# The down projections of a two-layer encoder: eleven chunk pairs by seven products instead of two whole chunks and ten pairs

## The chip, the cores and the metric

One core of a Trainium2 chip runs the whole program in one launch. The metric is the device time of one execution in microseconds (us). The engines are named as in the profile: PE is the matrix engine (PEld its weight loads), DVE the vector engine, ACT the scalar engine, POOL the GpSimd engine; SP issues most DMA transfers, POOL issues those that add into their target.

## The reference

Two layers over 512 tokens of width 1024. Each layer has two gated feed-forward half steps, a mixer between them (banded and dilated attention in the even layer, neighbourhood attention in the odd one), and a gated per-layer input at its end; a last norm follows.

```python
D_MODEL = 1024; SEQ = 512; DEPTH = 2; D_FF = 2816
def swiglu(x, w_gate, w_up, w_down):
    return (jax.nn.silu(x @ w_gate) * (x @ w_up)) @ w_down
...
for i in range(DEPTH):
    h = h + 0.5 * swiglu(rmsnorm(h, norm_ffn1[i]), ffn1_w_gate[i], ffn1_w_up[i], ffn1_w_down[i])
    hn = rmsnorm(h, norm_mix[i])
    h = h + (ab_mixer(hn, ...) if i % 2 == 0 else c_mixer(hn, ...))
    h = h + 0.5 * swiglu(rmsnorm(h, norm_ffn2[i]), ffn2_w_gate[i], ffn2_w_up[i], ffn2_w_down[i])
    gate = jax.nn.sigmoid(rmsnorm(h, norm_ple[i]) @ w_ple_gate[i])
    h = h + gate * (p[i] @ w_ple_proj[i])
return rmsnorm(h, norm_final)
```

All is float32. The change concerns the last matrix product of `swiglu`, 512 x 2816 by 2816 x 1024, which occurs four times. These four places are called the down stages here.

## The kernel before

**Number format.** A float32 operand is split into a high and a low part (`split`, lines 152 to 154): ACT copies it to the narrower matmul type (line 153) and DVE subtracts that copy from it (line 154). A product of two operands is then three matmuls: high by high, high by low, low by high. Each of them has a 128 x 128 stationary operand and here 512 moving columns. So every weight tile costs one ACT copy and one DVE subtraction before PE can use it. In the profile a split weight tile is `wh` and `wl`, a raw one is `wr` (1024 columns, 512 KB) or `tmp` (512 columns, 256 KB), an activation is `act`.

**A feed-forward half step.** `ffn` makes the 22 chunks of 128 hidden features: two in `front`, then four in each of five calls of `block`. `block` leaves its rows with tokens on the partitions; `turn_back` transposes them on PE (line 449) and ACT copies each transposed chunk out of its bank (line 450) into the list `a`. A block's chunks are turned during the next block (`between`), those of the last block inside the down stage (`turn`).

**The down stage** (`down`) multiplies the 22 chunks with the down weights. Of the 22, the first `WHOLE = 2` are multiplied plainly (`xs`, the weight halves `left` and `right`). The other 20 make `K2 = 10` pairs `A[k]`, `B[k]`. A pair is a 2 x 2 block product: tokens in two halves `l` and `r` of 256, the pair's two chunks, and the 1024 outputs in two halves of 512, so the weights of all pairs are four quarters `b11`, `b12`, `b21`, `b22`. Seven products stand in the place of eight, at the price of sums and differences of the operands and results: `inner_sums` (lines 496 to 498) and line 594 on the activations; on the weights the DMAs that add (`add`, line 533) and DVE adds in `summed` (line 567). One product of one pair is six matmuls: two banks of 128 tokens, three each.

Pairs go in units of two (`units`), five units before. The products are named `first` to `seventh`. Each unit's weights pass through a chain: `first` uses `b11`, then `b12` is added in place for `fifth`; later `summed` loads `b12` plus `b22` for `seventh`, `b11` is added for `sixth`, `b21` for `fourth`. `second` uses `b21` and `third` uses `b22`, loaded into `tmp` tiles (`halved`). The stage runs in this order:

- the whole chunks' right half for tokens `r` into the two transposition banks (`rx`); their weights and splits were prepared in the last block (`late`);
- a loop over the units `s`: `first(s)`, `second(s)`, and from `s = 2` on `fifth(s - 2)`. At `s = 1` the last four chunks are turned, through the two score banks, two around `second(1)` and two behind it;
- `summed(0)`, `seventh(0)`, the whole chunks' left half for tokens `l`, `summed(1)`, the last two `fifth`, the left half for tokens `r`;
- a loop `s = 1` to 6: `summed(s + 1)`, `seventh(s)`, `sixth(s - 1)`, `fourth(s - 2)`, at `s = 2` the whole chunks' right half for tokens `l`, at the end `third(0)`;
- `third(1)` to `third(4)`, between them the transposition of finished quarters, the addition to the residual (lines 683 and 693) and the split of the next norm's input (`norm_split`, lines 216 and 217); the last quarter follows `third(4)` (line 707 and line 693). The next stage's products read these splits.

**Order.** The instructions of an engine stand in the order of a scheduler that goes by the order of the program text, by which tile slots are free and by its own estimate of when operands are ready; so products can stand interleaved or be moved ahead. `issue_after(x)` keeps what it encloses behind `x` on `x`'s engine. `high_priority` moves instructions ahead. Each engine then runs its own list strictly in order. Slots: five `wr`, ten `tmp`, four `wh` and four `wl` tiles, 64 `act` tiles; PSUM has three `mm` banks, two `sc`, two `tr`, one `ob`.

Of the kernel before, what the change touches and what calls it, by code (L numbers as in the profile page):

```python
# [10 lines left out]
F32R = mybir.dt.float32r  # L11
# [4 lines left out]
P = 128  # L16
# [20 lines left out]
WHOLE = 2  # L37
READY = 8
K2 = (NF - WHOLE) // 2
# [16 lines left out]
class Trunk:  # L56
# [259 lines left out]
    def block(self, w, y, t, between, late, start):  # L316
# [90 lines left out]
        def fifth():  # L407
            for i in both:
                tt(base[i], base[i], chain[i], op=ALU.add)  # L409
            late()  # L410
# [43 lines left out]
    def ffn(self, i, which, k_next):  # L454
# [6 lines left out]
        a, xs, x1, sums, begin = [], [None] * WHOLE, [None] * K2, [None] * K2, []  # L461
# [3 lines left out]
        def between():  # L465
            a.extend(self.turn_back(rows, self.tbank))
            for k in range(READY):
                if WHOLE + 2 * k + 2 <= len(a) and sums[k] is None:
                    sums[k] = self.inner_sums(*a[WHOLE + 2 * k:WHOLE + 2 * k + 2])

        def late():
            if j == BLOCKS - 1:
                for n, x in enumerate(a[:WHOLE]):
                    xs[n] = self.split_chunk(x, nc.vector)
                for k in range(WHOLE):
                    begin.append(self.tmp())
                    nc.sync.dma_start(begin[k], dn[:, (WHOLE + k) * T:(WHOLE + k + 1) * T])

        for j in range(BLOCKS):
            n = 4 * UNIT + j * 8 * UNIT  # L480
            rows = self.block(gu[:, n:n + 8 * UNIT], y, t, between, late, first and j == 0)
        self.begin_norm(k_next)
        p = lambda: [self.per_layer(i, c) for c in range(2)]
        self.down(dn, a, xs, x1, sums, begin, kept, p if which == 2 else None, lambda n: a.extend(self.turn_back(rows, self.sbank, n)))
# [16 lines left out]
    def down(self, w, a, xs, x1, sums, begin, kept, inner, turn):  # L501
# [7 lines left out]
        A, B = _Step(a, WHOLE), _Step(a, WHOLE + 1)  # L509
        left, right = (w[:, n * WHOLE * T:(n + 1) * WHOLE * T] for n in range(2))  # L510
        b11, b12, b21, b22 = (w[:, 2 * WHOLE * T:][:, n * K2 * T:(n + 1) * K2 * T] for n in range(4))
        units = [range(u, min(u + 2, K2)) for u in range(0, K2, 2)]
        wide = [range(u, u + 2) for u in range(0, WHOLE, 2)]
# [39 lines left out]
        r1, r2 = [self.bank(), self.bank()], [self.bank(), self.obank()]  # L553
# [3 lines left out]

        rx = [self.tbank(), self.tbank()]
        for u in wide:
            product(rx, u, halved(right, u, begin[u.start:u.stop]), xs, r, True, u.stop == WHOLE)  # L560

        def summed(s):
            raws[s] = load(b12, units[s])
            for j, k in enumerate(units[s]):
                x, more = raws[s][:, j * T:(j + 1) * T], self.tmp()
                nc.sync.dma_start(more, b22[:, k * T:(k + 1) * T])
                tt(x, x, more, op=ALU.add)

# [11 lines left out]
        def second(s):  # L580
            u = units[s]
            for k in u:
# [1065 lines left out]
```

## Time and profile before

| | |
|---|---|
| three runs | 2004.49, 2005.36, 2005.66 us; median 2005.36 |
| the profiled execution | 2005.77 us; its span from first to last instruction 2003.9 us |
| mean granted PE clock | 0.997 |
| busy | PE 1976.0, PEld 1646.1, DVE 1537.0, ACT 1213.0, POOL 324.7 us |
| matmuls | 9726 |
| DMA | 346.12 MB, mean 173 GB/s |

Times inside the profile count from the first instruction of the span. A row of the timeline gives start, duration, engine, line, operation, tiles, shape and count; in brackets at its end stands how long the engine sat idle before it and what ended that. Consecutive matmuls overlap in their durations (0.39 us each for 512 columns), so what one costs PE is read from the distance of their starts. The same holds, less strongly, for DVE and ACT. The four down stages begin at 230.0, 859.1, 1251.7 and 1817.2 us.

### The profile page before, as it was taken

What the parts mean: (1) busy time and instruction counts of PE and PEld (TensorE: products, weight loads), DVE (VectorE), ACT (ScalarE), POOL (GpSimd) and SP (SyncE); (2) the same over time, 40 slices, a digit from 0 to 9 for tenths busy, and PEclk for the clock granted to TensorE, in tenths of its full rate; (3) what the DMA queues carried; (4) which work ended last, traced back from release to release, by engine and by line L of the source; (5) the groups of instructions that cost most, each with busy time, mean ns of one, the idle gap of its engine ahead of it and who ended that gap; (6) DMA issues with size and microseconds to landing.
All of it is one profiled execution on the core that took longest, in us unless ns stands there. A gap on an engine that the chain in (4) does not pass through costs nothing.

```text
span 2003.9 us, 28013 instructions
## 1 busy us (share of the span) xinstructions
PE 1976.0 (99%) x9726; PEld 1646.1 (82%) x9726; DVE 1537.0 (77%) x2648; ACT 1213.0 (61%) x2051; POOL 324.7 (16%) x378
## 2 busy tenths in 40 slices
PE   9999999999999999999999999999999999999997
PEld 7888788879888888878888888788888888887886
DVE  7787897798767677797786778877888668778775
ACT  7656765477645565675566556745766556666553
POOL 1111011341211221111122110011000122110111
PEclk9999999999999999999999999999999999999999
DMA  9877687543426787878568786785343577776961
GB/s 274 196 198 174 170 213 225 141 95 78 96 73 221 173 184 173 195 188 222 189 214 186 178 190 168 209 212 162 104 129 100 188 181 188 176 173 177 230 222 43
DMA packets 151069, 346.12 MB, mean 173 GB/s; under 512 B 26384, under 2 KB 34064, under 8 KB 150928
## 3 DMA queue, kind: packets, MB, share of 16 engines
q1 hardware_dynamic: 112704, 236.28, 36.0%
q0 software_dynamic: 38080, 108.02, 30.5%
q8 instruction: 76, 1.25, 0.2%
q14 instruction: 65, 0.53, 0.1%
q10 hardware_dynamic: 144, 0.04, 0.0%
HBM read 315.96 MB, written 17.27 MB: 166 GB/s over the span
## 4 chain that ended last, share of the span: by engine, by line
PE 87%; DVE 5%; DMA 3%; issue 3%; ACT 2%; POOL 0%; DVEq 0%; ACTq 0%; POOLq 0%
PE mm L368 7%; PE mm L369 7%; PE mm L367 7%; PE mm L178 5%; PE mm L180 5%; PE mm L179 5%; PE sc L367 3%; PE sc L369 3%; PE sc L368 3%; PE mm L544 3%; PE mm L542 3%; PE mm L543 3%; PE sc L543 2%; PE sc L544 2%; PE sc L542 2%
## 5 line engine op out<-in xcount | busy, mean ns | idle before, releaser
L153 ACT ACTIVATE wh<-wr 128x1024 fp32r<-128x1024 f32 (+1 forms) x408 | 427.2, 1050 | 424.2 <-DMA wr<-in_gu_dram 82.3
L154 DVE TENSOR_TENSOR wl<-wr,wh 128x1024 fp32r<-128x1024 f32 (+1 forms) x408 | 496.2, 1219 | 199.5 <-ACT wh L153 197.0
L367 PE MATMUL mm<-wh,act 128*128 128x512 f32 x640 | 250.9, 392 | 0.0
L369 PE MATMUL mm<-wh,act 128*128 128x512 f32 x640 | 250.7, 392 | 0.0
L368 PE MATMUL mm<-wl,act 128*128 128x512 f32 x640 | 249.5, 390 | 0.6 <-DVE wl L154 0.5
L153 ACT ACTIVATE wh<-tmp 128x512 fp32r<-128x512 f32 x264 | 155.6, 625 | 95.8 <-PE sc L369 32.6
L178 PE MATMUL mm<-act,wh 128*128 128x512 f32 (+1 forms) x472 | 184.8, 393 | 0.4 <-ACT act L153 0.4
L179 PE MATMUL mm<-act,wh 128*128 128x512 f32 (+1 forms) x472 | 184.5, 391 | 0.0
L180 PE MATMUL mm<-act,wl 128*128 128x512 f32 (+1 forms) x472 | 184.4, 391 | 0.0
L154 DVE TENSOR_TENSOR wl<-tmp,wh 128x512 fp32r<-128x512 f32 x264 | 171.5, 683 | 4.1 <-ACT wh L153 3.7
L337 POOL DMA_DIRECT2D wr<-in_gu_dram x80 | 80.4, 1020 | 379.8 <-DVE wl L154 360.6
L368 PEld LDWEIGHTS mm<-wl,act 128*128 128x128 f32 x640 | 120.2, 188 | 25.7 <-DVE wl L154 1.5
L369 PEld LDWEIGHTS mm<-wh,act 128*128 128x128 f32 x640 | 120.2, 188 | 24.4
L367 PEld LDWEIGHTS mm<-wh,act 128*128 128x128 f32 x640 | 120.3, 188 | 23.8
L154 DVE TENSOR_TENSOR act<-act,act 128x512 fp32r<-128x512 f32 (+1 forms) x216 | 133.8, 634 | 3.8 <-ACT act L153 3.7
L153 ACT ACTIVATE act<-act 128x512 fp32r<-128x512 f32 (+1 forms) x216 | 120.7, 582 | 24.0 <-DVE act L311 9.9
L367 PE MATMUL sc<-wh,act 128*128 128x512 f32 x320 | 124.6, 389 | 1.6 <-DVE act L291 1.6
L369 PE MATMUL sc<-wh,act 128*128 128x512 f32 x320 | 124.7, 390 | 0.0
L368 PE MATMUL sc<-wl,act 128*128 128x512 f32 x320 | 124.5, 389 | 0.0
L409 DVE TENSOR_TENSOR wr<-wr,wr 128x1024 f32<-128x1024 f32 x40 | 49.0, 1225 | 87.8 <-DMA wr<-in_gu_dram 87.6
L533 POOL DMA_DIRECT2D wr<-in_dn_dram x60 | 51.9, 864 | 365.9 <-DVE wl L154 325.3
L345 POOL DMA_DIRECT2D tmp<-in_gu_dram x80 | 74.8, 1200 | 221.8 <-DVE act L498 137.0
(272 smaller groups left out, 4631.3 us busy)
## 6 DMA issues: line engine op xcount, KB each, us to landing
wr<-in_gu_dram SPq DMA_DIRECT2D x92, 512.0 KB, 5.2
tmp<-in_gu_dram SPq DMA_DIRECT2D x160, 256.0 KB, 3.7
wr<-in_gu_dram POOLq DMA_DIRECT2D x80, 512.0 KB, 7.6
tmp<-in_dn_dram SPq DMA_DIRECT2D x144, 256.0 KB, 4.0
wr<-in_dn_dram POOLq DMA_DIRECT2D x60, 512.0 KB, 6.3
tmp<-in_gu_dram POOLq DMA_DIRECT2D x80, 256.0 KB, 5.9
wr<-in_dn_dram SPq DMA_DIRECT2D x40, 512.0 KB, 4.4
act<-kept SPq DMA_DIRECT2D x56, 256.0 KB, 4.5
```

What stands on the lines that cost most here:

```text
L153: self.put(self.nc.scalar.activation(hi, src, AF.Copy))
L154: self.put((lo_eng or self.nc.vector).tensor_tensor(lo, src, hi.bitcast(F32), op=ALU.subtract))
L178: mm(out, stat[0], mov[0], start=start, stop=False)
L179: mm(out, stat[0], mov[1], start=False, stop=False)
L180: return mm(out, stat[1], mov[0], start=False, stop=stop)
L337: nc.gpsimd.dma_start(raw, q[:, u * UNIT:(u + 1) * UNIT], accum_op=ALU.add)
L367: mm(p, xh, wh, start=start and k == 0, stop=False, skip_group_check=True)
L368: mm(p, xh, wl, start=False, stop=False, skip_group_check=True)
L369: self.last_mm = mm(p, xl, wh, start=False, stop=stop and k == half - 1, skip_group_check=True)
L542: mm(p, xh, wh, start=start and k == 0, stop=False, skip_group_check=True)
L543: mm(p, xh, wl, start=False, stop=False, skip_group_check=True)
L544: ins = mm(p, xl, wh, start=False, stop=stop and k == u.stop - 1, skip_group_check=True)
```

## The change

All 22 chunks become pairs: `WHOLE` is gone, `K2` is 11, and there are six units, the last with a single pair. With the whole chunks go `late`, `begin`, `xs`, `rx`, `left`, `right` and their products. `READY` goes from 8 to 9: the inner sums of pairs 0 to 8 are made during the blocks.

`second` now splits only the token half `l` of `B[k]` (`half_split`, 256 columns), and half `r`, which `fourth` needs, is split later, just ahead of `sixth` in the second loop. The split of the inner sums and line 594's addition move from `seventh` into `inner_split`, called one step ahead. The first `seventh` stands in the first loop, behind the last `second`; `summed(0)` and `summed(1)` stand behind `fifth(1)` and `fifth(2)`. The last chunks are turned at `s = 2`, through the transposition banks, the second two kept behind the end of `second(2)`. `fourth` starts its banks, `r3` is taken at the beginning of the stage. `third(0)` and `third(1)` stand in steps 3 and 4 of the second loop, `third(2)` behind `sixth(5)`, and `third(3)` to `third(5)` in the last loop, whose fourth pass then holds two `first_half` alone.

```diff
--- before.py
+++ after.py
@@ -34,9 +34,8 @@
 PLAIN = 2
 BLOCKS = (NF - PLAIN) // 4
 STAT_AT = 5
-WHOLE = 2
-READY = 8
-K2 = (NF - WHOLE) // 2
+READY = 9
+K2 = NF // 2
 ACTS = 64
 TMPS = 10
 WR = 5
@@ -313,7 +312,7 @@
         stt(t4, t2, -1.0, b21, op0=ALU.mult, op1=ALU.subtract)
         return [self.split_chunk(x, nc.vector) for x in (s, r)]
 
-    def block(self, w, y, t, between, late, start):
+    def block(self, w, y, t, between, start):
 
 
         nc, H, half = self.nc, T // 2, KC // 2
@@ -407,7 +406,6 @@
         def fifth():
             for i in both:
                 tt(base[i], base[i], chain[i], op=ALU.add)
-            late()
             product(A, base, t12, r, False, False)
             add(base, q3)
             with self.tc.high_priority():
@@ -458,30 +456,22 @@
         gu, dn = io[f"gu{which}"][i], io[f"dn{which}"][i]
         first = i == 0 and which == 1
         kept = io["xT"].rearrange("p c t -> c p t") if first else self.put_away()
-        a, xs, x1, sums, begin = [], [None] * WHOLE, [None] * K2, [None] * K2, []
+        a, x1, sums = [], [None] * K2, [None] * K2
         rows, t = self.front(gu, first)
         y = self.xg
 
         def between():
             a.extend(self.turn_back(rows, self.tbank))
             for k in range(READY):
-                if WHOLE + 2 * k + 2 <= len(a) and sums[k] is None:
-                    sums[k] = self.inner_sums(*a[WHOLE + 2 * k:WHOLE + 2 * k + 2])
-
-        def late():
-            if j == BLOCKS - 1:
-                for n, x in enumerate(a[:WHOLE]):
-                    xs[n] = self.split_chunk(x, nc.vector)
-                for k in range(WHOLE):
-                    begin.append(self.tmp())
-                    nc.sync.dma_start(begin[k], dn[:, (WHOLE + k) * T:(WHOLE + k + 1) * T])
+                if 2 * k + 2 <= len(a) and sums[k] is None:
+                    sums[k] = self.inner_sums(*a[2 * k:2 * k + 2])
 
         for j in range(BLOCKS):
             n = 4 * UNIT + j * 8 * UNIT
-            rows = self.block(gu[:, n:n + 8 * UNIT], y, t, between, late, first and j == 0)
+            rows = self.block(gu[:, n:n + 8 * UNIT], y, t, between, first and j == 0)
         self.begin_norm(k_next)
         p = lambda: [self.per_layer(i, c) for c in range(2)]
-        self.down(dn, a, xs, x1, sums, begin, kept, p if which == 2 else None, lambda n: a.extend(self.turn_back(rows, self.sbank, n)))
+        self.down(dn, a, x1, sums, kept, p if which == 2 else None, lambda n: a.extend(self.turn_back(rows, self.tbank, n)))
 
     def per_layer(self, i, c):
 
@@ -498,7 +488,7 @@
         tt(s[:, l], s[:, r], b[:, r], op=ALU.add)
         return s
 
-    def down(self, w, a, xs, x1, sums, begin, kept, inner, turn):
+    def down(self, w, a, x1, sums, kept, inner, turn):
 
 
 
@@ -506,11 +496,9 @@
         l, r = slice(0, H), slice(H, T)
         self.kept = self.dp.tile([KC, P, T], F32, name=self.nm("kept"))
         copy, tt, sub = nc.scalar.activation, nc.vector.tensor_tensor, ALU.subtract
-        A, B = _Step(a, WHOLE), _Step(a, WHOLE + 1)
-        left, right = (w[:, n * WHOLE * T:(n + 1) * WHOLE * T] for n in range(2))
-        b11, b12, b21, b22 = (w[:, 2 * WHOLE * T:][:, n * K2 * T:(n + 1) * K2 * T] for n in range(4))
+        A, B = _Step(a, 0), _Step(a, 1)
+        b11, b12, b21, b22 = (w[:, n * K2 * T:(n + 1) * K2 * T] for n in range(4))
         units = [range(u, min(u + 2, K2)) for u in range(0, K2, 2)]
-        wide = [range(u, u + 2) for u in range(0, WHOLE, 2)]
 
         def load(b, u):
             raw = self.wr.tile([P, UNIT], F32, tag="wr", name=self.nm("wr"))[:, :len(u) * T]
@@ -550,14 +538,10 @@
                 copy(o, x, AF.Copy)
             return out
 
-        r1, r2 = [self.bank(), self.bank()], [self.bank(), self.obank()]
+        r1, r2, r3 = [self.bank(), self.bank()], [self.bank(), self.obank()], [self.sbank(), self.sbank()]
         x2, x3, x4 = ([None] * K2 for _ in range(3))
         n, raws, marks = len(units), {}, []
         last = lambda u: u.stop == K2
-
-        rx = [self.tbank(), self.tbank()]
-        for u in wide:
-            product(rx, u, halved(right, u, begin[u.start:u.stop]), xs, r, True, u.stop == WHOLE)
 
         def summed(s):
             raws[s] = load(b12, units[s])
@@ -565,6 +549,16 @@
                 x, more = raws[s][:, j * T:(j + 1) * T], self.tmp()
                 nc.sync.dma_start(more, b22[:, k * T:(k + 1) * T])
                 tt(x, x, more, op=ALU.add)
+
+        def half_split(x):
+            t = self.act(F32R)
+            self.split(x, t[:, l], t[:, r])
+            return t[:, l], t[:, r]
+
+        def inner_split(s):
+            for k in units[s]:
+                x3[k] = self.split_chunk(sums[k], nc.vector)
+                tt(B[k][:, l], B[k][:, l], sums[k][:, r], op=ALU.add)
 
         def first(s):
             u = units[s]
@@ -579,9 +573,8 @@
 
         def second(s):
             u = units[s]
-            for k in u:
-                x2[k] = self.split_chunk(B[k], nc.vector)
-            product(r2, u, halved(b21, u), x2, l, True)
+            low = {k: half_split(B[k][:, l]) for k in u}
+            return product(r2, u, halved(b21, u), low, l, True, last(u))
 
         def fifth(s):
             u = units[s]
@@ -589,9 +582,6 @@
 
         def seventh(s):
             u = units[s]
-            for k in u:
-                x3[k] = self.split_chunk(sums[k], nc.vector)
-                tt(B[k][:, l], B[k][:, l], sums[k][:, r], op=ALU.add)
             product(rb, u, self.parts(raws[s]), x3, l, True, last(u))
             add(raws[s], b11, u)
 
@@ -602,60 +592,59 @@
 
         def fourth(s):
             u = units[s]
-            product(rc, u, self.parts(raws[s]), x2, r, False, last(u))
+            product(rc, u, self.parts(raws[s]), x2, l, True, last(u))
             for k in u:
-                t = self.act(F32R)
-                x4[k] = t[:, l], t[:, r]
-                self.split(B[k][:, l], *x4[k])
+                x4[k] = half_split(B[k][:, l])
 
         for s in range(n):
             first(s)
-            if s == 1:
+            if s == 2:
                 turn(range(2))
-            second(s)
-            if s == 1:
-                turn(range(2, 4))
-                r3 = [self.sbank(), self.sbank()]
-                c5 = copied(rx)
+            ins = second(s)
+            if s == 2:
+                with self.tc.issue_after(ins.ins):
+                    turn(range(2, 4))
+            if s == n - 1:
+                inner_split(0)
+                c11 = copied(r1)
+                rb = [self.tbank(), self.tbank()]
+                seventh(0)
             if s > 1:
                 fifth(s - 2)
-        c11 = copied(r1)
-        rb = [self.tbank(), self.tbank()]
-        summed(0)
-        seventh(0)
-        ws = [halved(left, u) for u in wide]
-        for u, ww in zip(wide, ws):
-            product(r2, u, ww, xs, l, False, u.stop == WHOLE)
-        summed(1)
+            if n - 4 < s < n - 1:
+                summed(s + 3 - n)
         for o, p in zip(c11, r2):
             tt(o, p, o, op=ALU.add)
         fifth(n - 2)
         fifth(n - 1)
-        rc = [self.bank(), self.obank()]
-        for u, ww in zip(wide, ws):
-            product(rc, u, ww, xs, r, True)
-        for o, p in zip(c5, r3):
-            tt(o, p, o, op=ALU.add)
+        c5, rc, done = copied(r3), [self.bank(), self.obank()], 0
+
         def third(i):
             u = units[i]
             product(r3, u, halved(b22, u), x4, l, False, last(u))
 
+        inner_split(1)
         for s in range(1, n + 2):
             if s + 1 < n:
                 summed(s + 1)
             if s < n:
                 seventh(s)
+            if s + 1 < n:
+                inner_split(s + 1)
             if s <= n:
+                for k in units[s - 1]:
+                    x2[k] = half_split(B[k][:, r])
                 sixth(s - 1)
             if s > n:
-                third(0)
+                third(done)
+                done += 1
             if s > 1:
                 fourth(s - 2)
+            if 2 < s < n - 1:
+                third(done)
+                done += 1
             if s == 2 and inner:
                 self.p = inner()
-            if 2 <= s < 2 + len(wide):
-                u = wide[s - 2]
-                product(r3, u, halved(right, u), xs, l)
             if s == n:
                 c2 = copied(r1)
                 u3 = [self.act(), self.act()]
@@ -694,9 +683,10 @@
                 self.h[m + j] = h
                 self.norm_split(m + j, c)
 
-        for i in range(n):
-            if i:
-                third(i)
+        rest = n - done
+        for i in range(max(rest, 4)):
+            if i < rest:
+                third(done + i)
             if i < 2:
                 second_half(M + 2 * i, c22, r)
             elif i < 4:
@@ -1528,10 +1518,7 @@
 
 def _quarters(w):
 
-    c = w.reshape(NF, P, 2, T)
-    whole = c[:WHOLE].transpose(1, 2, 0, 3).reshape(P, -1)
-    pairs = c[WHOLE:].reshape(K2, 2, P, 2, T).transpose(2, 1, 3, 0, 4).reshape(P, -1)
-    return np.concatenate([whole, pairs], axis=1)
+    return w.reshape(K2, 2, P, 2, T).transpose(2, 1, 3, 0, 4).reshape(P, -1)
 
 
 def _rows(w):
```

## The prediction

> **What bounds the kernel now.** I read the busy table first, then the busy time of the first down stage, then PE's timeline in it.
>
> ```profile
> PE 1976.0 (99%) x9726; PEld 1646.1 (82%) x9726; DVE 1537.0 (77%) x2648; ACT 1213.0 (61%) x2051; POOL 324.7 (16%) x378
> core 0: 2003.9 us, clock 0.997
> 230.00:343.30 113.30, 111.55 (x509) 91.69 (x508) 90.74 (x140) 68.39 (x107) 13.77 (x17) 1.00 0.80 204
> 230.03 0.39 PE L542 MATMUL tr<-wh,act 128*128 128x512 f32 x1
> 240.68 0.40 PE L544 MATMUL mm<-wh,act 128*128 128x512 f32 x1
> 240.91 1.04 PE L449 MATMUL sc<-ident,act 128*128 128x128 f32 x8
> 242.13 1.06 ACT L450 ACTIVATE act<-sc 128x512 f32<-128x512 f32 x2
> 242.76 1.14 PE L449 MATMUL sc<-ident,act 128*128 128x128 f32 x8 [0.81 <-ACT act L450]
> 248.18 0.39 PE L542 MATMUL sc<-wh,act 128*128 128x512 f32 x1
> 249.51 0.74 PE L544 MATMUL mm<-wh,act 128*128 128x512 f32 x2 [0.94 <-DVE act L154]
> 878.72 0.73 PE L544 MATMUL mm<-wh,act 128*128 128x512 f32 x2 [1.05 <-DVE act L154]
> 1270.89 0.73 PE L544 MATMUL mm<-wh,act 128*128 128x512 f32 x2 [0.59 <-DVE act L154]
> 1837.87 0.73 PE L544 MATMUL mm<-wh,act 128*128 128x512 f32 x2 [2.11 <-DVE act L154]
> 1839.20:1842.60 3.40, 3.40 (x10) 2.61 (x9) 3.07 (x6) 1.58 (x4) 0.86 (x1) 0.50 0.56 90
> ```
>
> PE is the bound everywhere, down stages included: in 113.3 us it idles 1.75 us. Windows list PE, PEld, DVE, ACT and POOL busy time, then the clock. From the start at 230.03 to that at 240.68 lie 47 steps without a gap, so a matmul costs 10.65 / 47 = 0.2266 us. A product of one unit (12 matmuls) is 2.72 us.
>
> The two gaps of the first stage stand in brackets, and each returns in all four stages:
>
> ```profile
> PE sc L449 <- ACT act L450: 3.2, 4, 0.8
> PE mm L544 <- DVE act L154: 4.7, 4, 2.1
> DVE wr L567 <- DMA wr<-in_dn_dram: 14.2, 8, 3.3
> 245.62 0.42 DVE L496 TENSOR_TENSOR act<-act,act 128x256 f32<-128x256 f32 x1
> 248.16 0.69 DVE L567 TENSOR_TENSOR wr<-wr,tmp 128x512 f32<-128x512 f32 x1 [2.12 <-DMA wr<-in_dn_dram]
> 248.77 0.69 DVE L154 TENSOR_TENSOR act<-act,act 128x512 fp32r<-128x512 f32 x1
> 243.50 4.57 DMA wr<-in_dn_dram
> ```
>
> The first is turning: 16 transposes stand together, and the second eight wait until ACT has emptied the two score banks. The second is line 567, the addition of `summed(0)`. The scheduler put it early; DVE, in order, idled 2.12 us in front of it for a load that the chain of waits shows from 243.50, right after the split that freed its slot; behind it stood the split that PE needed. In the fourth stage the gap was 2.11 us, and soon after the granted clock was 0.50 for 3.4 us: another 1.7 us lost.
>
> **The change part by part.** Sums are made against the profiled execution, 2005.77 us (span 2003.9), 0.41 above the median of the runs.
>
> *Matmuls.* Before, a stage has 2 x 24 + 10 x 42 = 468, after 11 x 42 = 462. Four stages save 24 x 0.2266 = 5.4 us: **-5.4**. PE has no other engine's cover to fall into, so this counts whole.
>
> *Turning.* After, the second eight transposes stand behind `second(2)`, 2.72 us later at least, and ACT's two copies cost 1.06 (the L450 row). The added wait on PE holds up only the inner sums of pair 10, needed two steps on. **-3.2** (bounds 0 and -3.2).
>
> *The load for `summed(0)`.* Only the fifth raw slot changes hands: four are taken by units 0 to 3, and `summed(0)` now stands ahead of unit 4's load, so it gets a slot that is free before the stage instead of the one `fifth(0)` frees. Its 4.57 us then pass under the first steps. But the loads of unit 4, `summed(1)` and unit 5 now wait for the slots of `fifth(0)`, `fifth(1)` and `fifth(2)`. Unit 5 is the tight one: slot, load, ACT and DVE split, `first(5)`, while PE has one product (2.72) between, plus the lead of the splits over PE (four `wh` tiles, at most three products, 8.2).
>
> ```profile
> wr<-in_dn_dram SPq DMA_DIRECT2D x40, 512.0 KB, 4.4
> wr<-in_dn_dram POOLq DMA_DIRECT2D x60, 512.0 KB, 6.3
> L533 POOL DMA_DIRECT2D wr<-in_dn_dram x60 | 51.9, 864 | 365.9 <-DVE wl L154 325.3
> 227.25 1.22 DVE L154 TENSOR_TENSOR wl<-wr,wh 128x1024 fp32r<-128x1024 f32 x1
> 228.38 0.68 DVE L154 TENSOR_TENSOR act<-act,act 128x512 fp32r<-128x512 f32 x1
> 228.99 0.68 DVE L154 TENSOR_TENSOR wl<-tmp,wh 128x512 fp32r<-128x512 f32 x1
> 229.59 1.33 DVE L436 TENSOR_TENSOR act<-mm,act 128x512 f32<-128x512 f32 x2
> 244.95 0.75 DVE L594 TENSOR_TENSOR act<-act,act 128x256 f32<-128x256 f32 x2
> ```
>
> 4.4 plus two half-unit splits of some 0.6 is 5.6, so a lead of 3 us covers it. The gain is between 0 and 4.7 + 1.7 = 6.4. Of the eight DMA waits of line 567 four cost PE nothing, so most of it should stay gained; I let 0.5 per stage come back, near the smallest of the four gaps (0.59): **-4.4**.
>
> *DVE's work in all.* Start to start a 1024-column subtraction takes 1.13 us (227.25 to 228.38), 512 columns 0.6, 256 columns 0.335 (two from 244.95 to 245.62). Splitting by halves makes three 0.335 of one 0.6 and one 0.335: +0.07 per pair. The eleventh pair costs seven weight halves, one sum of weights, two chunk splits (ten times 0.6, 6.0), and seven operations of 256 columns (2.3). Gone are two whole chunks' splits, six halves of their weights and two additions of results (6.0). Net +3 us per stage against 113.3 - 90.74 = 22.6 us idle: nothing, except in the tail below. ACT and POOL (three more adding transfers a stage at 0.86, idle 365.9 before the old ones) have more room; DMA grows by some 2 MB of 346. The six-step chain of adds keeps its distances, 8.2 us and more from `sixth` to `fourth` against 6.3 plus splits, as before; for the single pair the last is 6.8 with half the transfer.
>
> *Inner sums a step ahead* change an order, not a number: 0. Steps 1 and 2 of the second loop ask 6.0 and 7.8 us of DVE under 5.4 and 8.2 of PE; the three `fifth` ahead (6.8 of PE, 2.8 of DVE) lend the missing 0.6. The whole chunks' products, which lent 5.4 there, are gone: without that lead, 0.6 a stage.
>
> *Start of the stage.* The whole chunks' 12 matmuls were a cover in front of `first(0)`. Its operands were ready by 229.1 (228.38 and its duration), before 230.03; but its banks come from the block, and line 436 reads two of them until 230.9. One `mm` bank is free earlier, and the second is needed only 0.68 after the first. Bounds 0 and +0.9 a stage; 0.2 taken: **+0.8**.
>
> *Third products.* Two are moved into steps 3 and 4 with their loads (two of 256 KB each on SP), ACT copies and 1.2 us of DVE. There DVE has room:
>
> ```profile
> 294.00:310.00 16.00, 16.00 (x72) 13.28 (x71) 10.23 (x13) 8.65 (x13) 3.46 (x4) 1.00 0.89 200
> 310.00:326.00 16.00, 16.00 (x73) 13.23 (x72) 8.00 (x10) 8.44 (x14) 0.87 (x1) 1.00 0.75 170
> 322.10:343.30 21.20, 21.20 (x106) 17.49 (x105) 18.89 (x32) 14.02 (x25) 1.68 (x3) 1.00 0.63 206
> 327.09 3.69 DVE L154 TENSOR_TENSOR wl<-tmp,wh 128x512 fp32r<-128x512 f32 x6
> 331.90 1.28 DVE L154 TENSOR_TENSOR wl<-tmp,wh 128x512 fp32r<-128x512 f32 x2
> 351.31 0.47 DVE L217 SCALAR_TENSOR_TENSOR act<-act,gain,act 128x256 fp32r<-128x256 f32 x1
> 351.85 0.39 PE L178 MATMUL ob<-act,wh 128*128 128x512 f32 x1
> ```
>
> But they leave the tail. From the last `sixth` (322.1) to the next stage's first product (343.3) PE had seven products; now 60 matmuls, 13.6 us, 5.4 less. DVE worked 18.89 of those 21.2 us and loses three weight halves (eight stand there now), half a `fourth` split, and gains a quarter split: 16.9 in a window of 15.8. It ends 1.1 us late if it uses all its 2.3 us of idle time, 3.4 if none. The end of the chain has 0.3 us of slack: the last low part is ready at 351.78 and the second matmul behind 351.85 reads it. So 0.8 to 3.1 us a stage; where the per-layer gate follows (stages two and four), 12 matmuls on `p` that need no norm can fill 2.7 of it. I take 2.0 twice and 0.4 twice: **+4.8**.
>
> Sum: -5.4 - 3.2 - 4.4 + 0.8 + 4.8 = -7.4, so 1998.4 for that execution, 1998.0 against the median.
>
> A weighing: the trace has the clock at 0.50 after a gap of 2.11 us, not after 1.05. The Trainium skill, "TensorE: Matmul & The Clock Gate", What's actually happening, puts the throttled state behind an idle window of about 3.4 us; the trace was stricter, and by the skill the third term would lack its 1.7.
>
> **Rivals.**
>
> - *Everything is hidden:* the tail's idle time on DVE is used and the waits stay away: -5.4 - 3.2 - 6.4 = -15.0, 1990.4. For it: DVE's idle time ahead of the tail; against: 0.3 us of slack.
> - *The DMA wait only moves* (the change doesn't do there what it says): DVE or ACT stands before unit 5's load or `summed(1)` as it stood before `summed(0)`. All 6.4 come back: -3.0, 2002.4, within 0.2%. For it: eight such waits now.
> - *The tail turns the sign:* DVE uses none of the idle time, 3.1 us in all four stages (12.4), and each such gap, over 2.11, brings 3.4 us at half clock (6.8): -5.4 - 3.2 - 4.4 + 0.8 + 19.2 = +7.0, 2012.4. It decides from 2 us a gap on. Against it: the scheduler fills PE with what is ready.
> - *The same gaps at full clock:* without the 6.8, +0.2, 2005.6. The window of about 3.4 us in that section of the Trainium skill would give this one.
>
> **How the numbers follow.** My forecast (1993 to 2003) 0.50; all hidden 0.18; the wait moves 0.17; the sign turns 0.10; gaps at full clock 0.05. A measurement here tells 0.2%, 4.0 us, from no change. Faster: 0.47 of the first, all of the second: 0.65; same 0.25; slower 0.10. The range 1990 to 2006 leaves out the slower case and a little of the second.
>
> **What would show it.** 1848 matmuls in lines of `product`; no row of L449 waiting for L450; L567 without a wait in the first steps; PE gaps behind the last `third`, ended by L217 or L216. It would be wrong if PE waits in the second loop for splits by DVE, which I cost at nothing, or if `first(5)` waits for its load.

## The result, and the profile after

The changed kernel took 2024.98 us (four runs, 2016.86 to 2031.11) against 2004.92 for the kernel before on the same chip: ratio 1.0099, 95% interval 1.0084 to 1.0114. It is 1% slower. The prediction had it faster, at 1998.0 us (1990 to 2006): neither the direction nor the time is right. The profiled execution of after took 2031.11 us (span 2029.3), the slowest of its four and 6 us above their median; its runs spread over 0.7%, those of before over 0.1%.

The busy row of after's page:

```profile
PE 1983.8 (98%) x9702; PEld 1643.9 (81%) x9702; DVE 1551.5 (76%) x2716; ACT 1221.9 (60%) x2107; POOL 334.6 (16%) x390
```

The windows of after: the whole first down stage, then 8 to 12 us in the middle of each of the four (columns as before: PE, PEld, DVE, ACT, POOL busy time, granted clock, DMA share, GB/s):

```profile
230.60:344.70 114.10, 110.55 (x487) 89.39 (x485) 89.24 (x144) 67.40 (x114) 14.69 (x17) 0.99 0.80 203
284.00:292.00 8.00, 5.16 (x16) 3.83 (x17) 4.30 (x7) 4.48 (x8) 1.31 (x2) 0.79 1.05 241
921.00:930.00 9.00, 6.80 (x19) 5.05 (x18) 6.27 (x10) 6.67 (x12) 0.86 (x1) 0.62 1.07 240
1321.00:1330.00 9.00, 5.25 (x16) 4.18 (x17) 5.45 (x9) 5.98 (x10) 0.86 (x1) 0.81 1.05 221
1890.00:1902.00 12.00, 6.71 (x21) 4.76 (x20) 6.84 (x11) 4.18 (x9) 2.50 (x3) 0.72 1.01 217
```

There are 24 matmuls fewer, as counted, and two third products fewer behind the last `sixth`; still the stage is 0.8 us longer than before (114.1 against 113.3, from its first product to the end of its last third). Behind that the next stage's first product, which followed at once in before (343.31), starts 4.5 us later (349.21). In the four short windows PE starts 72 matmuls, worth 72 x 0.2266 = 16.3 us, in 38 us: 21.7 us are lost there. PE's table of waits for the whole run names what ended the idle time:

```profile
PE tr L530 <- ACT act L152: 13.6, 4, 4.5
PE tr L666 <- DVE act L682: 2.8, 2, 1.4
PE tr L666 <- DVE act L672: 2.5, 8, 0.3
PE tr L532 <- DVE act L153: 2.5, 4, 0.8
```

Gone are both rows that the prediction read in before, the wait for the turning copies and that behind line 567. In their place stands a wait once per stage for ACT, with a small one for DVE just ahead of it, and the waits for the `turned` transposes (L666) in the tail. The timeline around the new wait, PE's rows, then ACT's, then DVE's:

```profile
283.94 0.50 PE L532 MATMUL tr<-wh,act 128*128 128x512 f32 x1 [0.70 <-DVE act L153]
287.98 0.80 PE L530 MATMUL tr<-wh,act 128*128 128x512 f32 x1 [2.84 <-ACT act L152]
288.57 0.63 PE L531 MATMUL tr<-wl,act 128*128 128x512 f32 x1
...
280.63 1.06 ACT L538 ACTIVATE act<-sc 128x512 f32<-128x512 f32 x2
281.58 0.63 ACT L152 ACTIVATE act<-act 128x512 fp32r<-128x512 f32 x1
286.35 1.06 ACT L152 ACTIVATE wh<-wr 128x1024 fp32r<-128x1024 f32 x1 [4.14 <-DMA wr<-in_dn_dram]
287.31 2.79 ACT L152 ACTIVATE act<-act 128x512 fp32r<-128x512 f32 x6
...
276.17 1.29 DVE L551 TENSOR_TENSOR wr<-wr,tmp 128x512 f32<-128x512 f32 x2 [2.18 <-issue]
277.38 1.22 DVE L153 TENSOR_TENSOR wl<-wr,wh 128x1024 fp32r<-128x1024 f32 x1
```

The chain of waits has the transfer in front of ACT's split (start, length, what):

```profile
278.89 7.38 DMA wr<-in_dn_dram
```

Read backwards: PE needs the high part of the fourth pair's inner sum (`x3[3]`). ACT does it at 287.41, at once behind the weight split of `sixth(1)`. That split stood 4.14 us for the adding transfer of `b11`, which took 7.38 us and could start only when `seventh(1)`'s low part was off DVE (277.38 and its 1.22); and DVE had first idled 2.18 us at line 551, the sum for the *next* unit ("issue": the profile names no releaser; its operands come by transfers). `x3[2]`, the pair before, is made at 281.58, behind `c5`'s copies of the last `fifth` (L538): in the text `inner_split(1)` stands behind them. After the gap the matmuls take 0.63 and follow each other at 0.43 us, half clock.

ACT's wait alone does not explain the loss. The table of waits of ACT for 275 to 323 us, in before and then in after:

```profile
ACT wh L153 <- DMA wr<-in_dn_dram: 19.3, 7, 4.2
ACT wh L152 <- DMA wr<-in_dn_dram: 4.1, 1, 4.1
```

Before, ACT stood longer for these transfers, up to 4.2 us at one split, and PE waited nowhere in that stretch. So what counts is what stands behind the blocked split, and how soon PE needs it.

The tail of the first stage, PE's and then DVE's rows:

```profile
346.23 1.29 PE L666 MATMUL tr<-ident,act 128*128 128x128 f32 x8 [1.41 <-DVE act L682]
347.80 0.66 PE L666 MATMUL tr<-ident,act 128*128 128x128 f32 x4 [0.28 <-DVE act L672]
...
340.91 1.23 DVE L153 TENSOR_TENSOR wl<-wr,wh 128x1024 fp32r<-128x1024 f32 x1 [1.49 <-ACT wh L152]
344.12 1.23 DVE L153 TENSOR_TENSOR wl<-wr,wh 128x1024 fp32r<-128x1024 f32 x1 [1.65 <-ACT wh L152]
```

The last third product ends near 344.7; 16 of the transposes come after it, and the groups wait for DVE to empty a bank. Ahead of that, DVE had idled 1.49 and 1.65 us at weight splits of the next part of the kernel.

### The profile page after: what moved, and what is told of

It reads as the page before. It is cut to its first block, busy times and chain, and to the rows that moved or that the text cites. A ratio compares the mean times of both kernels' runs of the same rounds, so it can differ in the third digit from the quotient of the medians.

```text
span 2029.3 us, 28142 instructions
## 1 busy us (share of the span) xinstructions
PE 1983.8 (98%) x9702; PEld 1643.9 (81%) x9702; DVE 1551.5 (76%) x2716; ACT 1221.9 (60%) x2107; POOL 334.6 (16%) x390
## 4 chain that ended last, share of the span: by engine, by line
PE 74%; DVE 8%; DMA 8%; issue 7%; ACT 3%; POOL 1%; DVEq 0%; POOLq 0%; ACTq 0%
PE mm L367 6%; PE mm L368 5%; PE mm L366 5%; PE mm L179 5%; PE mm L178 5%; PE mm L177 5%; DMA wr<-in_gu_dram 4%; PE sc L366 3%; PE sc L368 3%; PE sc L367 3%; DVE wl L153 3%; PE mm L531 2%; DMA wr<-in_dn_dram 2%; PE mm L532 2%; PE mm L530 2%
## 5 line engine op out<-in xcount | busy, mean ns | idle before, releaser
L152 ACT ACTIVATE wh<-wr 128x1024 fp32r<-128x1024 f32 (+1 forms) x428 | 438.8, 1030 | 455.1 <-DMA wr<-in_gu_dram 85.0
L153 DVE TENSOR_TENSOR wl<-wr,wh 128x1024 fp32r<-128x1024 f32 (+1 forms) x428 | 509.9, 1196 | 214.2 <-ACT wh L152 211.5
L152 ACT ACTIVATE wh<-tmp 128x512 fp32r<-128x512 f32 x248 | 146.7, 625 | 81.6 <-PE sc L368 32.6
L153 DVE TENSOR_TENSOR wl<-tmp,wh 128x512 fp32r<-128x512 f32 x248 | 161.7, 685 | 4.7 <-ACT wh L152 4.2
L153 DVE TENSOR_TENSOR act<-act,act 128x512 fp32r<-128x512 f32 (+1 forms) x268 | 138.4, 554 | 6.1 <-ACT act L152 5.9
L521 POOL DMA_DIRECT2D wr<-in_dn_dram x72 | 62.2, 864 | 389.6 <-DVE wl L153 377.3
```

The lines of the kernel that those rows point to most:

```text
L152: self.put(self.nc.scalar.activation(hi, src, AF.Copy))
L153: self.put((lo_eng or self.nc.vector).tensor_tensor(lo, src, hi.bitcast(F32), op=ALU.subtract))
L521: nc.gpsimd.dma_start(raw, b[:, u.start * T:u.stop * T], accum_op=ALU.add)
```

## The experiments

The theory: splits of inner sums stand, on the two engines that work in order, behind instructions that wait for transfers (middle), and too few thirds are left to cover the transposes (tail). The rival: ACT and DVE have too much to do there, and any gap that is removed comes up elsewhere. Times are medians; the kernel before took 2006.31, 2005.53, 2006.58, 2005.71 and 2005.41 us beside the five groups (e1 to e4, e5 to e7, e8 to e10, e11 and e12, e13 to e16) and 2004.92 beside after, so a difference between kernels of different groups is uncertain by some 1 to 2 us. e4, e8, e10, e13 and e14 leave out part of the sums and so compute something else; they are there for their time alone.

### Split ahead, thirds last, and both

```diff
e1:  +        inner_split(1)
              c5, rc, done = copied(r3), [self.bank(), self.obank()], 0
     ...
     -        inner_split(1)
e2:  -            if 2 < s < n - 1:
     -                third(done)
     -                done += 1
e3:  both
```

> One line is moved: the first call of inner_split in the second half (unit 1) stands ahead of the copies of r3 instead of behind them. Theory A (text order): act tiles are given out in the order of the text, so the splits of unit 1's inner sums wait behind the copies of r3, which wait for the last fifth on PE; then the next split on ACT stands behind a load that is still adding. Under A the gap of 2.4 to 4.6 us in the middle of each stage and the half clock behind it go, some 20 to 26 us in all: 1999 to 2006 us. Theory B (lost cover): the whole chunks' products were 5.4 us of PE work with little DVE work at this place, and without them DVE cannot keep up; then the order of a line is worth under 5 us: 2019 or more.

> The two third products of steps 3 and 4 go back to the end of the stage (one behind the last sixth, five in the last loop); all else as changed. Theory C (tail): with only three third products at the end, PE runs out before DVE has finished the quarters, 1.8 to 3.2 us a stage; back at the end they cover it: 10 us less, 2011 to 2016. Rival D: the tail's gaps come from the two first_half pairs that stand behind the last third, and the thirds' place does not matter: 2021 or more. The gap in the middle stays in both.

> Both edits of the two runs before: the split of unit 1's inner sums ahead of the copies of r3, and all third products at the end. Under A and C together all the new stalls are gone and the matmuls (5.4), the turning (3.2 to 3.9) and the wait for the load of summed(0) (5 to 7) stay saved: 1988 to 1994. Under B and D: 2015 or more.

Measured: 2011.45 us (ratio 1.0025, 1.0014 to 1.0035), 2014.24 (1.0044, 1.0030 to 1.0057) and 2003.88 (0.9991, 0.9982 to 1.0000). One moved line is worth 13.5 us of after's 2024.98, the thirds' place 10.7, both 21.1 (by the ratios to before 14.8, 11.0 and 21.7). PE's waits in the first stage of e1:

```profile
PE tr L666 <- DVE act L682: 1.4, 1, 1.4
...
PE tr L532 <- DVE act L153: 0.6, 1, 0.6
PE tr L530 <- ACT act L152: 0.3, 1, 0.3
```

The longest of e2:

```profile
PE tr L530 <- ACT act L152: 3.4, 1, 3.4
```

And of e3:

```profile
PE mm L531 <- DVE wl L153: 1.1, 2, 0.8
PE tr L532 <- DVE act L153: 0.6, 1, 0.6
PE tr L530 <- ACT act L152: 0.2, 1, 0.2
```

Each edit takes its own stall and leaves the other's (e1 keeps the tail's row, e2 the 3.4 us): both places are shown to cost time. e2 falls into its range. But e1 and e3 miss theirs, e3 by 10 us: there is a third cost. In e3 ACT stands 4.10 us at the same split (row below), now with `x3[5]` behind it, and PE waits for low parts of weights (`wl`).

### The adding transfer, in after and in e3

```diff
e4 (after):  -            add(raws[s], b11, u)
             +            if s != 1:
             +                add(raws[s], b11, u)
e8 (e3):     -            add(raws[s], b11, u)
```

> Order and slots as changed, but the adding transfer of b11 for unit 1 is left out, so sixth(1) multiplies b12 plus b22 instead of b11 plus b12 plus b22. Then ACT does not stand before that transfer, but the splits of unit 1 still come late. Theory A with both halves: the first short gap (0.4 to 0.9) stays, the long one falls from 2.4 to 4.6 us to about 1, and the half clock goes: 2004 to 2012. If the text order alone were the cause: 2020 or more. If the transfer alone were: below 2002.

> The kernel with both edits (split ahead, thirds last) took 2003.9 us and still loses about 2.5 us per down stage in three places of the second loop (some 1.2 near 287, 0.5 near 298, 0.8 near 320 in stage 1, ten in all). This kernel is that one with every adding transfer of b11 in the second loop left out, so that the sixth products multiply b12 + b22 alone; matmuls, splits and DVE's adds are all there. A (what is left is the same chain: ACT stands at a weight split until the adding transfer has landed, and what is queued behind comes in a burst): the places go, 1992 to 1997. B (DVE and ACT simply have too much to do there): DVE's and ACT's work is unchanged, 2001 to 2005.

Measured: 2006.76 us (1.0007, 0.9998 to 1.0016) and 1990.74 (0.9927, 0.9914 to 0.9941). Without one transfer per stage after is 18 us faster, as expected for the two halves together. Without all of them, that for `sixth(0)` included, e3 is 13 us faster, 1.3 us below the range of A, and PE's table of waits is empty for the first stage. DVE and ACT still do all their splits there, which speaks against the rival. What these runs can't tell apart is ACT's wait and the traffic: both go with the transfer.

### The sums of b22

```diff
e10 (e3):    -            for j, k in enumerate(units[s]):
             -                x, more = raws[s][:, j * T:(j + 1) * T], self.tmp()
             -                nc.sync.dma_start(more, b22[:, k * T:(k + 1) * T])
             -                tt(x, x, more, op=ALU.add)
e13 (e3):    -                x, more = raws[s][:, j * T:(j + 1) * T], self.tmp()
             -                nc.sync.dma_start(more, b22[:, k * T:(k + 1) * T])
             -                tt(x, x, more, op=ALU.add)
             +                x = raws[s][:, j * T:(j + 1) * T]
             +                tt(x, x, x, op=ALU.add)
e14 (e3):    -                tt(x, x, more, op=ALU.add)
             +                tt(x[:, :8], x[:, :8], more[:, :8], op=ALU.add)
```

> The kernel with both edits, with b22's loads and DVE's adds of them (two of 0.68 us per unit) left out, so that the seventh products multiply b12 alone; the adding transfers stay. A (the chain): only some of what stands near 298 and 320 can go, 2000 to 2004. B (DVE's work): 1993 to 1998, since eleven adds and eleven loads per stage are gone.

> The kernel with both edits (2003.9 us), with b22's eleven loads per stage for the sums left out and DVE's adds kept (each piece of b12 is added to itself). W (what matters is DVE's wait for b22's load, and the traffic of 512 KB per unit beside the adding transfers): as without sums, 1989 to 1995. V (what matters is DVE's time, eleven adds of 0.68 us per stage): 2001 to 2006.

> The counterpart: b22's loads stay, and DVE adds only the first 8 of 512 columns of each, so that it still waits for each load and has next to no work. W: 2000 to 2005, as with the whole adds. V: 1990 to 1996.

Measured: 1990.81 us (0.9927, 0.9914 to 0.9939), 1995.27 (0.9946, 0.9932 to 0.9959) and 2005.22 (0.9995, 0.9986 to 1.0004). The first is what the rival expected, and with it alone I would have blamed DVE. The other two, each 0.2 to 0.3 us above the range of W, tell the loads from the adds: without b22's loads 8.6 us of e3's 2003.88 go, and with loads but hardly any adding nothing. Once the loads are away, the adds make 4.5 us (e13 against e10, whose intervals overlap a little). The timeline of e3: DVE at the sums, POOL's adding transfer, ACT's split of `sixth(1)`:

```profile
276.05 0.69 DVE L551 TENSOR_TENSOR wr<-wr,tmp 128x512 f32<-128x512 f32 x1 [1.85 <-issue]
277.86 1.22 DVE L153 TENSOR_TENSOR wl<-wr,wh 128x1024 fp32r<-128x1024 f32 x1
279.38 0.86 POOL L521 DMA_DIRECT2D wr<-in_dn_dram  x1 [10.22 <-DVE wl L153]
285.93 1.06 ACT L152 ACTIVATE wh<-wr 128x1024 fp32r<-128x1024 f32 x1 [4.10 <-DMA wr<-in_dn_dram]
```

The same places in e10:

```profile
274.09 1.23 DVE L153 TENSOR_TENSOR wl<-wr,wh 128x1024 fp32r<-128x1024 f32 x1
275.61 0.86 POOL L521 DMA_DIRECT2D wr<-in_dn_dram  x1 [7.25 <-DVE wl L153]
281.21 1.06 ACT L152 ACTIVATE wh<-wr 128x1024 fp32r<-128x1024 f32 x1 [0.23 <-DMA wr<-in_dn_dram]
```

In e3 DVE idles in front of the sum for unit 2 (1.85 us), with `seventh(1)`'s low part behind it; POOL's add is issued 3.77 us later than in e10, and ACT's wait grows from 0.23 to 4.10.

That DVE waits there for b22's load is not shown. In e13, which has no such load, DVE idles nearly as long at the same sum, and the profile names the load of b12:

```profile
274.85 0.69 DVE L550 TENSOR_TENSOR wr<-wr 128x512 f32<-128x512 f32 x1 [1.55 <-DMA wr<-in_dn_dram]
```

What e13 does change is how soon the adding transfers land. The table of DMA issues for 275 to 325 us, in e3, e13 and before (the last number is the median time to landing):

```profile
wr<-in_dn_dram POOLq DMA_DIRECT2D x9, 512.0 KB, 6.8
...
wr<-in_dn_dram POOLq DMA_DIRECT2D x9, 512.0 KB, 5.9
...
wr<-in_dn_dram POOLq DMA_DIRECT2D x9, 512.0 KB, 7.3
```

They land most slowly in before, where PE does not wait for them. So slow landing alone does not explain e3's loss either.

### Order alone

```diff
e11 (e3):    seventh(s) ahead of summed(s + 1) in the text, and
             +                with self.tc.issue_after(lo.ins):   # seventh's low part on DVE
                                  tt(x, x, more, op=ALU.add)
e12 (e3):    the same behind the low part of sixth(s - 1)
e15, e16 (e11, e12):
             +            if s == n - 1:
             +                third(done)
             +                done += 1
```

> The kernel with both edits (split ahead, thirds last; 2003.9 us), and DVE's adds of b22 for the unit of the next step are ordered behind DVE's part of the seventh product's weight split instead of ahead of it; nothing is left out. In the kernel with both edits DVE stood 1.85 us at such an add, whose load had not landed, with the split of seventh(1) behind it (277.86 against 274.09 in the kernel without b22's sums), so that the adding transfer of b11 was issued 3 us or more later and ACT waited 4.1 us for it. Theory (one chain: b22's load, DVE's add, DVE's split behind it, the adding transfer, ACT's split behind that): the adds of unit 1 and 2 are issued 3 us earlier and the waits go, as in the kernel without sums: 1991 to 1997. Rival (each of the two experiments that left something out only gave DVE and DMA less to do): 2000 to 2005.

> The same, with the adds of b22 one place later still: behind DVE's part of the weight split of the sixth product of the same step. By the theory the first stretch is as in the other kernel, 1991 to 1997; the sums now come just ahead of the next seventh product, so a late one would show as a wait for the weights of the seventh product: up to 2002. By the rival 2000 to 2005.

> The kernel with the sums behind the seventh product's split (2008.5 us), and one third product moved from the end of the stage into the sixth step of the second loop, where ACT stood four times at a weight split for an adding transfer (2.8, 2.6, 0.4 and 2.6 us before 317) and PE lost 1.0 to 4 us. If time for the transfers is what lacks there, 2.7 us of PE's work in that place take these waits: 2000 to 2004. If the third only brings more traffic (256 KB twice), 2007 to 2012.

> The same third product in the kernel with the sums behind the sixth product's split (2004.2 us): its gaps of 1.0 to 2.4 us in the sixth step of three stages go, the ones near 291 stay: 1998 to 2002; with traffic as the cause 2004 to 2009.

Measured: 2008.54 us (1.0016, 1.0005 to 1.0026), 2004.19 (0.9992, 0.9983 to 1.0001), 2002.05 (0.9982, 0.9973 to 0.9991) and 2000.99 (0.9982, 0.9973 to 0.9991). In e11 POOL's add is issued at 275.23 and PE's waits near 287 are gone in the first stage, as the chain says; but later in the loop ACT still stands at one weight split after another, and the time is above even the rival's range; e12 falls into it. The theory of one chain does not hold for the time. ACT's waits for 275 to 323 us, in e3 and then in e11:

```profile
ACT wh L152 <- DMA wr<-in_dn_dram: 15.4, 7, 4.1
ACT wh L152 <- DMA wr<-in_dn_dram: 16.4, 8, 3.8
```

PE's waits in the four stages add up to 7.8 us in e3 and to 10.4 in e11.

One third product in the sixth step takes 6.5 and 3.2 us off, as expected if time for the transfers is what lacks there, and not as expected of more traffic. Both of these kernels leave nothing out and are 0.18% faster than before, with an interval that excludes 1; that is the edge of what can be told here. In the last one, one wait of PE for the low parts of `fourth(0)`'s weights is left per stage, 0.8 to 2.6 us, 1.99 in the first.

### Further ahead, and a third early

```diff
e5 (e3):     inner_split(1) and inner_split(2) ahead of c5; in the loop
             inner_split(s + 2) for inner_split(s + 1); one third in step n - 1
e9 (e3):     -                x4[k] = half_split(B[k][:, l])
             +                x4[k] = x4[k] or half_split(B[k][:, l])
     ...
             +            if s == 1:
             +                for k in units[0]:
             +                    x4[k] = half_split(B[k][:, l])
             +                third(done)
             +                done += 1
```

> From e3_both: the splits of the inner sums two steps ahead instead of one (units 1 and 2 ahead of the copies of r3), and one third product moved back into step 5, between sixth(4) and the single pair's sixth(5). What is left in e3's stages are gaps of 0.4 and 0.8 us (the next unit's splits stand on ACT behind a split that waits for an adding transfer) and two waits for low parts of weights, about 0.5 and 1.0 us (the adding chain, tightest for the single pair). Theory A (in-order ACT behind the adding transfers): with the splits ahead of them and a third as cover all four go, 8 to 10 us: 1994 to 1997. Theory B (DVE has too much work without the whole chunks as cover): the gaps move on to the next split, 2001 or more.

> The kernel with both edits, and one third product (pair 0 and 1 of b22) put behind the sixth product of the first step of the second loop, its operand split there. It gives the adding transfer of b11 that the second step waits for one product, 2.7 us, more, and takes one third out of the row at the end. A: the waits near 287 (1.2 us per stage) go and the rest stays, 1997 to 2001. B: the third brings its own splits into the crowded stretch and the waits move on, 2002 to 2008.

Measured: 2009.26 us (1.0016, 1.0007 to 1.0025) and 2008.21 (1.0009, 0.9999 to 1.0018); both went the rival's way (e9 0.2 us beyond its range). PE's waits in the first stage of e5:

```profile
PE mm L531 <- DVE wl L153: 1.4, 1, 1.4
PE tr L531 <- DVE wl L153: 1.3, 1, 1.3
```

ACT's row in e9:

```profile
285.91 1.06 ACT L152 ACTIVATE wh<-wr 128x1024 fp32r<-128x1024 f32 x1 [3.69 <-DMA wr<-in_dn_dram]
```

In e5 all inner sums pass in time; when the blocked split is through, ACT's arrears run in a burst, and PE waits for low parts of weights. In e9 the halves that the early third needs were written behind that same split, and PE stood 3.2 us for them (from 284.7 to 287.9): after's fault made again.

### The turning and the raw slot, in the kernel before

```diff
e6 (before): +                with self.tc.issue_after(ins.ins):   # end of second(1)
                                  turn(range(2, 4))
e7 (e6):     -WR = 5
             +WR = 6          # and ACTS = 62
```

> The kernel before, with one part of the change alone: the second eight transposes of the last chunks are kept behind the end of second(1). The four gaps of 0.97 us (start to start) between the two groups go: 3.2 to 3.9 us less, ratio 0.998. A rival: the scheduler puts something else into their place and PE waits there for DVE; then 0.

> As e6, with six raw weight slots (and 62 act tiles, to make room), so that the load of summed(0) gets a slot before the stage, as in the changed kernel. Without an eleventh pair. If the wait for that load was the cause of the gap of 0.75 to 2.3 us and of the half clock in one stage: another 5 to 7 us less, 1994 to 1997 in all. If DVE was late there by its own work: as e6.

Measured: 2011.16 us (1.0030, 1.0020 to 1.0040) and 2015.69 (1.0057, 1.0044 to 1.0069). Both are slower than the kernel before, which neither expectation allowed, and neither isolates its term. PE's rows of e6:

```profile
243.76 0.50 PE L542 MATMUL mm<-wh,act 128*128 128x512 f32 x1 [1.81 <-ACT act L153]
248.48 0.50 PE L542 MATMUL sc<-wh,act 128*128 128x512 f32 x1 [0.81 <-ACT act L450]
```

DVE's of e7:

```profile
251.34 1.29 DVE L567 TENSOR_TENSOR wr<-wr,tmp 128x512 f32<-128x512 f32 x2 [3.85 <-DMA wr<-in_dn_dram]
```

With the transposes apart, in e6, `second(1)` waits 1.81 us for a split that stands on ACT behind the turning copies, and the next product for its score banks. With a sixth slot DVE stands 3.85 us at the next sum: the rival that the wait only moves.

## Why the prediction was wrong

- **Matmuls, turning, the load for `summed(0)`: their waits are gone, as predicted.** With the load's half clock they make at most -15.0. The kernels in which PE waits nowhere in the first stage, e8 and e10, took 1990.74 and 1990.81 us, against 1990.4 for "everything is hidden" (they move less by DMA, so this is agreement and not proof). After has no PE wait in the first loop, `first(5)` included, and no trace isolates the three terms from each other (e6 and e7 do not). DVE's own waits at the sums did not all go: 9.0 us in four are left of 14.2 in eight, and one of the four is the 2.18 us ahead of the new stall. In that the rival "the DMA wait only moves" had a part.
- **Start of the stage:** PE goes from the block's last matmul at 230.35 to the first product at 230.58 without a gap; +0.8 was too much by 0.8.
- **"Inner sums a step ahead change an order, not a number: 0" failed.** I compared DVE's work with PE's in sums per step and did not follow the queue. The step puts ACT's splits behind `c5`'s copies and, by that, behind a split that waits for a transfer of 7.38 us. e1 measured the line's place at 13.5 us. The prediction named the symptom ("PE waits in the second loop for splits"), but for DVE, and at no price.
- **"The six-step chain of adds keeps its distances" was true and not enough.** In after PE waits only once, 0.6 us in the fourth stage, for a weight of the second loop. But the chain's waits stand in ACT's queue in front of other work, and that was priced at nothing. With both edits undone the chain still holds 13 us (e3 against e8 and e10). Before had ACT waits as long and slower transfers without a loss; what has gone since is the whole chunks' products, of which the prediction itself counted 5.4 us of PE's work at that place. That this cover is the cause is an argument: no run puts it back alone. e15 and e16, with 2.7 us more of PE's work in one step, speak for it.
- **The tail, +4.8, was mis-sized.** e2 gives 10.7 us. The mechanism was the predicted one (transposes and norms behind too few thirds), but DVE used none of its idle time: from 330.1 to 344.65 us it idled 4.0 us, all of it at weight splits, most of them of the next part. PE's waits there were mainly for L682 and L672 (5.3 us in the run), and only 1.2 us for L216, which was L217 in before. The window of the working also began 0.7 us late (before's last `sixth` ended at 321.4, not 322.1), so its lower bound was 0.1 and not 0.8 us a stage. Of the rival "the tail turns the sign" the price was nearly right (12.4 at full clock), the half clock was not: the tail's longest wait was 1.4 us, and none of after's four tails was at half clock.
- **What adds up:** the profiled executions differ by 2031.1 - 2005.8 = +25.3. -15.0 for the gains, +21.7 for the four windows, +1.7 for the small waits ahead of three of them and +10.7 for the tail give +19.1. 6 us stay unplaced; by the starts of the matmuls some 3 of them lie outside of the down stages, where the two kernels do the same. The 21.7 belong to the slowest execution and e1's 13.5 to medians, so they need not agree.

What stays open: what the 13 us that are left in e3 consist of. PE's table of waits names 7.8 of them. b22's loads and b11's adding transfers each take part, as e13 and e8 show; whether by their traffic, by the waits in the two queues or by the lost cover is not separated, and e11 shows that order alone is not enough.

## What to carry to other kernels

Price a moved step in the queue of the engine that runs it: list what stands ahead of it there, and above all any instruction that waits for a transfer; the sum of busy times per step says nothing about that. Where two engines in order pass work to a transfer and take it back, a wait ahead of the hand-over can come out larger behind it (DVE idle for 1.85 us at a sum, ACT then for 4.10 at a split). It costs nothing as long as no work that is needed soon stands behind it, as before showed. A cover that is moved forward must be counted at the place it leaves as well, with the idle time of the covering engine taken as used by nobody.

## What the hardware showed

In these traces the length of one wait of PE does not decide whether the half clock follows. It came after waits of 2.84 us (after) and 1.96 (e12, where the matmuls then follow each other at 0.43 us for 3.4 us), and in e1 in a tail with waits of 1.40 and 0.28. It did not come after 2.81 in e7 (nor after 1.99 in e16). The prediction's rule, half clock from 2 us a gap on, rested on two gaps and does not hold. "TensorE: Matmul & The Clock Gate" of the Trainium skill, What's actually happening, has an idle window of about 3.4 us; in these runs the half clock came after shorter waits. Rows and windows (the clock stands in the third column from the right) of e12, e1 and e7:

```profile
292.97 0.50 PE L532 MATMUL mm<-wl,act 128*128 128x512 f32 x1 [1.96 <-DVE wl L153]
290.00:299.00 9.00, 7.04 (x24) 5.34 (x23) 9.00 (x16) 6.56 (x14) 1.73 (x2) 0.81 0.67 147
...
1368.25 1.29 PE L666 MATMUL tr<-ident,act 128*128 128x128 f32 x8 [1.40 <-DVE act L682]
1369.75:1373.15 3.40, 3.33 (x13) 2.85 (x14) 3.40 (x8) 3.35 (x6) 1.69 (x3) 0.50 0.98 292
...
1852.03 0.49 PE L544 MATMUL mm<-wh,act 128*128 128x512 f32 x1 [2.81 <-DVE act L154]
1852.00:1855.50 3.50, 3.47 (x15) 2.88 (x16) 3.50 (x7) 1.08 (x3) 0.20 (x1) 1.00 0.83 131
```
